# Pieces of 128 columns for GpSimd's two-input operations in an RWKV-7 scan, and a group norm with three DVE operations fewer

## The chip, the cores and the metric

The kernel runs on one core of one Trainium2 chip. The metric is the device time of one execution in microseconds. Its engines are named as in the profile: PE (TensorE matmuls), PEld (TensorE weight loads), DVE (VectorE), ACT (ScalarE), POOL (GpSimd), SP (SyncE, which issues the DMAs).

## The reference

A trunk of two layers on 512 tokens of width 2048, in float32. Layer 0 (stick-breaking attention and a pooling mixer) is not touched. Layer 1 is an RWKV-7 time mixing with 32 heads of 64: projections r, k, v, g, a decay w and a rate a, then a recurrence over the tokens, then a group norm over each head's 64 values, a bonus, a gate and an output projection:

```python
def step(state, inp):
    r_t, w_t, k_t, v_t, kk_t, a_t = inp
    sa = jnp.einsum('bhvk,bhk->bhv', state, -kk_t)
    state = (state * w_t[:, :, None, :] + sa[..., None] * (kk_t * a_t)[:, :, None, :]
             + v_t[..., None] * k_t[:, :, None, :])
    return state, jnp.einsum('bhvk,bhk->bhv', state, r_t)
...
mean = jnp.mean(o, axis=-1, keepdims=True)
var = jnp.mean(jnp.square(o - mean), axis=-1, keepdims=True)
o = ((o - mean) * lax.rsqrt(var + GN_EPS)).reshape(B_, S, D) * gn_w + gn_b
bonus = jnp.sum(r * k * r_k, axis=-1, keepdims=True) * v
o = (o + bonus.reshape(B_, S, D)) * jax.nn.silu(g)
return o.astype(x.dtype) @ w_o
```

## The kernel before

The 32 heads are worked on as 16 pairs p; a pair fills the 128 partitions, two heads of 64. The recurrence is cut into 8 chunks of 64 tokens, so that a chunk becomes a few small matrix products and the state passes from chunk to chunk. All of this is in `scan`, which writes the instructions of several pairs interleaved:

- `vproj(p)` computes v of a pair on PE (vps, lines 142 to 144: 48 matmuls of 128x512 in three passes with split operands). Its weights come in four units of 128x512, loaded by `wunit` one unit ahead of their use. `split` turns each into a high part (whi, an ACT cast, line 137) and a low part (wlo = wraw - whi, line 138). From pair 2 on wlo is made by GpSimd, elsewhere by DVE.
- `gprod(p)` makes products of the loaded factors; DVE masks them into Z (line 885).
- `vprep(p)` multiplies v by the bonus on GpSimd (bv, line 900) and clears RS there (line 903).
- `lanes(p)` and `levels(p)` invert 64x64 triangular matrices. Four GpSimd multiplications gather 16x16 blocks out of Z (nd, line 920); a DVE transpose turns them (lt, line 925); then DVE runs 15 steps of a product pr (line 932, t x t columns in step t) and a reduction uc (line 933).
- `chain(p)` is the recurrence: per chunk PE makes xo, DVE and ACT copy it (xs, lines 1021 and 1022), PE makes sa, DVE copies it (RS, line 1026), PE makes s, and DVE makes the new state M (lines 1041 and 1043). ACT copies the output to O (line 1049).
- `post(p)` is the group norm and the gate of a pair: two reductions (lines 1061 and 1068) and tiny 128x8 operations around them (gs, lines 1062 and 1069; and in `rsqrt_eps`, lines 206 to 214: rssgn, rshgn, rstgn, rsygn), the scaling of O, a transpose on PE, the bonus and the gate (gm, lines 1080 and 1081).

The order is written by hand for PE: `slot` runs 12 steps of two chains (pairs p and p + 1) for each pair, and between the steps it takes from a list of due times (`plan`) the next part of the other generators. DVE, ACT, POOL and SP take their instructions in an order that a scheduler makes from this, with the chains first. Each engine runs its own instructions in order. On POOL the wlo stand in one queue with bv, the clearing of RS and the nd of later pairs.

Of the kernel before, what the change touches and what calls it, by code (L numbers as in the profile page):

```python
# [8 lines left out]
F32 = mybir.dt.float32  # L9
F32R = mybir.dt.float32r  # L10
I32 = mybir.dt.int32
AF = mybir.ActivationFunctionType
ALU = mybir.AluOpType
# [4 lines left out]
P = 128  # L18
# [6 lines left out]
GN_EPS = 64e-5  # L25
# [9 lines left out]
class Kernel:  # L35
# [96 lines left out]
                for n, f, at, r in g:  # L132
                    self.vec[n] = v[:, at:at + r]

    def split(self, hi, lo, src, eng=None):

        self.nc.scalar.copy(hi, src)  # L137
        (eng or self.nc.vector).tensor_sub(lo, src, hi.bitcast(F32))  # L138

    def mm3(self, ps, ah, al, bh, bl, start, stop):  # L140
        mm = self.nc.tensor.matmul
# [4 lines left out]
    def wunit(self, ap, a, b, pool=None, bufs=None, eng=None):  # L146

        pool = pool or self.wp
        ww = self.ww
        raw = self.wp.tile([P, ww], F32, tag="wraw", name="wraw", bufs=3)[:, :a * b].rearrange("p (a b) -> p a b", a=a)  # L150
        self.nc.sync.dma_start(raw, ap)
        kw = {"bufs": bufs} if bufs else {}
        hi = pool.tile([P, ww], F32R, tag="whi", name="whi", **kw)[:, :a * b].rearrange("p (a b) -> p a b", a=a)
        lo = pool.tile([P, ww], F32R, tag="wlo", name="wlo", **kw)[:, :a * b].rearrange("p (a b) -> p a b", a=a)
        self.split(hi, lo, raw, eng)
        return hi, lo

    def gemm_a(self, W, c0, xs, evac, kblocks=NK, feed=None):
# [39 lines left out]
            src = y  # L198
        return y

    def rsqrt_eps(self, pool, v, eps, n, name):

        nc = self.nc
        T = lambda tag: pool.tile([P, n], F32, tag=tag, name=tag + name, bufs=2)
        sd, hx, t, y = T("rss"), T("rsh"), T("rst"), T("rsy")
        nc.scalar.activation(sd, v, AF.Sqrt, bias=self.eps[eps])
        nc.vector.tensor_scalar(hx, v, eps, -0.5, ALU.add, ALU.mult)
        nc.vector.reciprocal(sd, sd)
        if n == 1:
            nc.vector.tensor_scalar(t, sd, sd, hx, ALU.mult, ALU.mult)  # L210
        else:
            nc.vector.tensor_mul(t, sd, sd)
            nc.vector.tensor_mul(t, t, hx)
        nc.vector.scalar_tensor_tensor(y, t, 1.5, sd, ALU.add, ALU.mult)
        return y
# [600 lines left out]
    def scan(self, ctx, xv, first, mp, ld, ar_d, bk_d, bc_d, g_d, m_d):  # L816
        nc, tc, i = self.nc, self.tc, self.i
# [8 lines left out]
        tp = ctx.enter_context(tc.tile_pool(name="stmp", bufs=1))  # L826
        Wv, Wo = i["od_w_v"][0], i["od_w_o"][0]
        lo, hi = slice(0, 64), slice(64, 128)
# [17 lines left out]
        def vproj(p):  # L846

            unit = lambda k0: self.wunit(
                Wv[k0 * P:(k0 + 4) * P, p * P:(p + 1) * P].rearrange("(k p) n -> p k n", p=P), 4, P,
                eng=nc.gpsimd if p > 1 else None)  # L850
            ws = first if p == 0 else [unit(0)]
            ps = pv.tile([P, S], F32, tag="v", name="vps")
            for k in range(NK):
                if k % 4 == 0:
                    wh, wl = ws.pop(0)
                    if k + 4 < NK and not ws:
                        ws.append(unit(k + 4))
                self.mm3(ps, wh[:, k % 4, :], wl[:, k % 4, :], xv[k][:, 0, :], xv[k][:, 1, :], k == 0, k == NK - 1)
                if k % 2 and k < NK - 1:
                    yield  # L860
            vT = sets[p]["vT"] = tp.tile([P, S], F32, tag="vT", name="vT")
            nc.scalar.copy(vT, ps)
            yield

        def gprod(p):

            s = sets[p]
            AR = s["AR"] = ld.tile([P, 8, 2, 64], F32, tag="AR", name="AR", bufs=4)
            nc.sync.dma_start(AR.rearrange("p a b c -> p (a b c)"), ar_d[p])
            BK = ld.tile([P, 8, P], F32, tag="BK", name="BK")  # L870
            nc.sync.dma_start(BK.rearrange("p a b -> p (a b)"), bk_d[p])
            yield

            Z = s["Z"] = [st.tile([P, 8, P], F32, tag=f"Z{h}", name=f"Z{h}", bufs=4) for h in range(2)]
            for b in range(2):
                g = [aux("g").rearrange("p (c n) -> p c n", c=4) for _ in range(2)]
                for c in range(4):
                    for h in range(2):
                        mm(g[h][:, c, :], BK[half[h], 4 * b + c, :],
                           AR[half[h], 4 * b + c].rearrange("p a b -> p (a b)"), start=True, stop=True)  # L880
                    if c == 1:
                        yield
                for h in range(2):
                    mk = self.mk[:, 64 * (p % 2):64 * (p % 2) + P]
                    nc.vector.tensor_mul(Z[h][:, 4 * b:4 * b + 4, :], g[h], mk.unsqueeze(1).to_broadcast([P, 4, P]))  # L885
                yield
            BT = s["BT"] = st.tile([P, 8, P], F32, tag="BT", name="BT")
            for b in range(2):
                g = aux("bt")
                for c in range(4):  # L890
                    nc.tensor.transpose(g[:, c * P:(c + 1) * P], BK[:, 4 * b + c, :], self.ident)
                nc.scalar.copy(BT[:, 4 * b:4 * b + 4, :], g.rearrange("p (c n) -> p c n", c=4))
                yield

        def vprep(p):

            s = sets[p]
            bv = s["bv"] = tp.tile([P, S], F32, tag="bv", name="bv", bufs=3)
            nc.sync.dma_start(bv, bc_d[p])
            nc.gpsimd.tensor_mul(bv, s["vT"], bv)  # L900

            RS = s["RS"] = st.tile([P, 8, 2, 64], F32, tag="RS", name="RS", bufs=3)
            nc.gpsimd.memset(RS[half[p % 2]], 0.0)
            yield
            g = aux("vt")
            for t in range(4):
                nc.tensor.transpose(g[:, t * P:(t + 1) * P], s["vT"][:, t * P:(t + 1) * P], self.ident)
            g5 = g.rearrange("p (t h n) -> p t h n", t=4, h=2)
            for par, rows in ((0, lo), (1, hi)):
                nc.scalar.copy(RS[half[1 - p % 2], par::2], g5[rows])  # L910
            yield
# [141 lines left out]
        def post(p):  # L1053

            s = sets[p]
            gt = tp.tile([P, S], F32, tag="ldg", name="ldg")
            nc.sync.dma_start(gt, g_d[p])
            O = s["O"].rearrange("p t h n -> p (t h) n")
            sm = tp.tile([P, 8], F32, tag="gs", name="gs")
            bc = lambda t: t.unsqueeze(2).to_broadcast([P, 8, 64])  # L1060
            nc.vector.tensor_reduce(sm, O, AX.X, ALU.add)
            nc.vector.tensor_scalar(sm, sm, 1.0 / 64, None, ALU.mult)
            yield
            nc.vector.tensor_sub(O, O, bc(sm))
            sq = tp.tile([P, 8, 64], F32, tag="pt", name="gsq")
            nc.scalar.activation(sq, O, AF.Square)
            yield
            nc.vector.tensor_reduce(sm, sq, AX.X, ALU.add)
            nc.vector.tensor_scalar(sm, sm, 1.0 / 64, None, ALU.mult)
            rs = self.rsqrt_eps(tp, sm, GN_EPS, 8, "gn")  # L1070
            yield
            nc.vector.tensor_mul(O, O, bc(rs))
            yield
            g = aux("ot")
            for t in range(4):
                nc.tensor.transpose(g[:, t * P:(t + 1) * P], s["O"][:, t].rearrange("p h n -> p (h n)"), self.ident)
            m = tp.tile([P, S], F32, tag="pt", name="gm")
            nc.scalar.activation(m, g, AF.Identity, scale=self.vec["gw"][:, p:p + 1], bias=self.vec["gb"][:, p:p + 1])
            yield
            nc.vector.tensor_add(m, m, s["bv"])  # L1080
            nc.vector.scalar_tensor_tensor(m, m, 0.5, gt, ALU.mult, ALU.mult)
            if p < 13:
                nc.sync.dma_start(m_d[p], m)
            else:
                t = mixed[p] = mp.tile([P, 2, S], F32R, tag="mx", name="mixed")
                self.split(t[:, 0, :], t[:, 1, :], m)
            yield
# [67 lines left out]
        def plan_pair(base, q, skip=0):  # L1155

            gp = gprod(q)
            next(gp)
            plan(base, gp, 6, *GP)
            plan(base, hurry(lanes(q)) if q == 15 else lanes(q), 18, *LA)  # L1160
            plan(base, hurry(levels(q)) if q == 15 else levels(q), 5, *LV)
            plan(base, vproj(q), 8, *VJ)
            plan(base, vprep(q), 2, *VP)


        v, gp = vproj(0), gprod(0)
# [9 lines left out]
        g1, v = gprod(1), vproj(1)  # L1176
        next(g1)
        run(la)
        for q in range(6):
            next(g1)  # L1180
            if q % 2:
                next(v)
        run(vprep(0))
        la, l0 = lanes(1), levels(0)
        for q in range(10):
# [122 lines left out]
```

## Time and profile before

| what | value |
|---|---|
| runs shown | 2131.53, 2136.67 and 2141.84 us, median 2136.67 |
| the profiled execution's own time | 2133.83 us |
| its span, first to last instruction | 2132.1 us |
| mean granted TensorE clock | 0.991 of full speed |
| layer 1's scan (first and last vps matmul of v to the last chain step) | about 1420 to 1960 us |

A span is read by stage: the shares of the whole span mix layer 0, the projections and the scan. In rows by line, "x15" is the count, then come the busy time in microseconds and the mean duration of one in nanoseconds, then the idle time of the engine just before these instructions and who ended it. In rows in order of time, a start and a length in microseconds stand first, and the idle time before in square brackets. The chain of waits is followed back from the last instruction, at each step to what released it.

### The profile page before, as it was taken

The numbers are of one execution on the slowest core, as the hardware profiler recorded it, in microseconds if no ns is written. First come the engines' busy times: TensorE is split into PE (matmuls) and PEld (weight loads), VectorE is DVE, ScalarE is ACT, GpSimd is POOL, SyncE is SP. The second block draws the span as 40 slices with busy tenths as digits, with TensorE's granted clock in tenths as the row PEclk, the third lists the DMA queues.
The fourth block names the chain that finished last, engine by engine and source line by source line (L and its number), as shares of the span: only waits on it lengthen the run. The fifth ranks groups of instructions, "written<-read, shape, count | busy, mean of one in ns | idle before, by whom it ended". The sixth has DMA issues, their size and how long they took to land. (4 is left out here: it accounts for less than half of the span.)

```text
span 2132.1 us, 33773 instructions
## 1 busy us (share of the span) xinstructions
PE 2036.6 (96%) x13139; PEld 1645.7 (77%) x13139; DVE 1301.0 (61%) x2557; ACT 954.4 (45%) x1663; POOL 268.9 (13%) x334
## 2 busy tenths in 40 slices
PE   8999999999999998999899989999999999989996
PEld 7888888888888897777688768876667676666786
DVE  5334335445333358666777793368888988987336
ACT  3345345333221138555555672254555555564211
POOL 0000000000000000333000030012333333310003
PEclk9999999999999999999999999999999999999998
DMA  5322222333333343455466665322222332333733
GB/s 190 99 70 79 82 77 65 94 99 99 99 105 113 127 170 123 147 177 157 130 235 215 211 210 189 122 80 63 91 87 89 105 104 68 104 109 100 232 104 114
DMA packets 214031, 262.97 MB, mean 123 GB/s; under 512 B 15768, under 2 KB 161776, under 8 KB 213104
## 3 DMA queue, kind: packets, MB, share of 16 engines
q1 hardware_dynamic: 213872, 260.83, 37.6%
q8 instruction: 103, 1.69, 0.3%
q14 instruction: 56, 0.46, 0.1%
HBM read 214.32 MB, written 46.47 MB: 122 GB/s over the span
## 5 line engine op out<-in xcount | busy, mean ns | idle before, releaser
L138 DVE TENSOR_TENSOR wlo<-wraw,whi 128x1024 fp32r<-128x1024 f32 (+1 forms) x268 | 313.8, 1173 | 487.5 <-ACT whi L137 478.5
L137 ACT CAST whi<-wraw 128x1024 fp32r<-128x1024 f32 (+1 forms) x324 | 303.5, 938 | 563.8 <-PE ga L143 318.7
L143 PE MATMUL ga<-mx,whi 128*128 128x512 f32 x768 | 301.9, 393 | 4.1 <-DVE mx L138 4.1
L142 PE MATMUL ga<-mx,whi 128*128 128x512 f32 x768 | 301.1, 393 | 4.5 <-ACT mx L137 4.5
L142 PE MATMUL ga<-x,whi 128*128 128x512 f32 x768 | 301.0, 392 | 0.0
L144 PE MATMUL ga<-mx,wlo 128*128 128x512 f32 x768 | 301.0, 392 | 0.0
L144 PE MATMUL ga<-x,wlo 128*128 128x512 f32 x768 | 299.5, 390 | 0.4 <-DVE wlo L138 0.4
L143 PE MATMUL ga<-x,whi 128*128 128x512 f32 x768 | 299.1, 390 | 0.0
L490 PE MATMUL gb<-wlo,mixed 128*128 128x512 f32 (+1 forms) x576 | 196.8, 343 | 3.1 <-DVE wlo L138 3.1
L488 PE MATMUL gb<-whi,mixed 128*128 128x512 f32 (+1 forms) x576 | 197.4, 343 | 1.8 <-DVE s L439 1.8
L489 PE MATMUL gb<-whi,mixed 128*128 128x512 f32 (+1 forms) x576 | 196.9, 342 | 0.0
L143 PEld LDWEIGHTS ga<-mx,whi 128*128 128x128 f32 x768 | 145.4, 189 | 38.0 <-DVE mx L138 6.9
L142 PEld LDWEIGHTS ga<-mx,whi 128*128 128x128 f32 x768 | 145.1, 189 | 37.9 <-ACT mx L137 5.9
L144 PEld LDWEIGHTS ga<-mx,wlo 128*128 128x128 f32 x768 | 145.3, 189 | 30.9 <-issue 0.3
L144 PEld LDWEIGHTS ga<-x,wlo 128*128 128x128 f32 x768 | 144.2, 188 | 31.2 <-DVE wlo L138 0.9
L142 PEld LDWEIGHTS ga<-x,whi 128*128 128x128 f32 x768 | 144.3, 188 | 29.4 <-ACT whi L137 0.3
L143 PEld LDWEIGHTS ga<-x,whi 128*128 128x128 f32 x768 | 144.3, 188 | 29.1
L490 PEld LDWEIGHTS gb<-wlo,mixed 128*128 128x128 f32 x576 | 109.1, 190 | 16.8 <-DVE wlo L138 4.4
L488 PEld LDWEIGHTS gb<-whi,mixed 128*128 128x128 f32 x576 | 109.1, 190 | 16.0 <-DVE s L439 3.5
L489 PEld LDWEIGHTS gb<-whi,mixed 128*128 128x128 f32 x576 | 109.2, 190 | 12.4
L142 PE MATMUL vps<-mx,whi 128*128 128x512 f32 x256 | 113.3, 443 | 0.0
L138 POOL TENSOR_TENSOR wlo<-wraw,whi 128x512 fp32r<-128x512 f32 x56 | 74.4, 1328 | 256.6 <-ACT whi L137 234.2
(330 smaller groups left out, 3401.0 us busy)
## 6 DMA issues: line engine op xcount, KB each, us to landing
wraw<-in_ev_w_in SPq DMA_DIRECT2D x96, 512.0 KB, 3.6
wraw<-in_ev_w_out SPq DMA_DIRECT2D x32, 512.0 KB, 3.6
wraw<-in_od_w_k SPq DMA_DIRECT2D x32, 512.0 KB, 4.9
wraw<-in_od_w_r SPq DMA_DIRECT2D x32, 512.0 KB, 4.5
wraw<-in_od_w_g SPq DMA_DIRECT2D x32, 512.0 KB, 3.4
wraw<-in_od_w_v SPq DMA_DIRECT2D x64, 256.0 KB, 2.8
ar_d<-pAR SPq DMA_DIRECT2D x16, 512.0 KB, 2.6
bk_d<-pBK SPq DMA_DIRECT2D x16, 512.0 KB, 3.3
```

What stands on the lines that cost most here:

```text
L137: self.nc.scalar.copy(hi, src)
L138: (eng or self.nc.vector).tensor_sub(lo, src, hi.bitcast(F32))
L142: mm(ps, ah, bh, start=start, stop=False)
L143: mm(ps, ah, bl, start=False, stop=False)
L144: mm(ps, al, bh, start=False, stop=stop)
L488: mm(ps, ah, bh, start=start, stop=False)
L489: mm(ps, al, bh, start=False, stop=False)
L490: mm(ps, ah, bl, start=False, stop=stop)
```

## The change

GpSimd's operations with two inputs in the scan are written as pieces of 128 columns: each wlo of the 56 units as four subtractions, and each bv as four multiplications. In the group norm the two scalings of the sums by 1/64 go: the mean's is folded into the centering, which becomes one scalar_tensor_tensor, and the variance's into the scale of the square root on ACT. The half variance rshgn moves from DVE to ACT. DVE loses three instructions of 128x8 per pair, 48 in all; ACT gains 16; POOL has 288 instructions where it had 72. PE's instructions and their order stay the same.

```diff
-    def split(self, hi, lo, src, eng=None):
+    def split(self, hi, lo, src, eng=None, parts=1):
         self.nc.scalar.copy(hi, src)
-        (eng or self.nc.vector).tensor_sub(lo, src, hi.bitcast(F32))
+        n = src.shape[1] // parts
+        for q in range(parts):
+            sl = slice(q * n, q * n + n)
+            (eng or self.nc.vector).tensor_sub(lo[:, sl], src[:, sl], hi[:, sl].bitcast(F32))
...
-        self.split(hi, lo, raw, eng)
+        self.split(hi, lo, raw, eng, a if eng else 1)
...
-    def rsqrt_eps(self, pool, v, eps, n, name):
+    def rsqrt_eps(self, pool, v, eps, n, name, scale=1.0):
...
-        nc.scalar.activation(sd, v, AF.Sqrt, bias=self.eps[eps])
-        nc.vector.tensor_scalar(hx, v, eps, -0.5, ALU.add, ALU.mult)
+        nc.scalar.activation(sd, v, AF.Sqrt, bias=self.eps[eps], scale=scale)
+        if n == 1:
+            nc.vector.tensor_scalar(hx, v, eps, -0.5, ALU.add, ALU.mult)
+        else:
+            nc.scalar.activation(hx, v, AF.Copy, bias=-0.5 * eps, scale=-0.5 * scale)
...
-            nc.gpsimd.tensor_mul(bv, s["vT"], bv)
+            for q in range(4):
+                nc.gpsimd.tensor_mul(bv[:, q * P:q * P + P], s["vT"][:, q * P:q * P + P], bv[:, q * P:q * P + P])
...
             nc.vector.tensor_reduce(sm, O, AX.X, ALU.add)
-            nc.vector.tensor_scalar(sm, sm, 1.0 / 64, None, ALU.mult)
             yield
-            nc.vector.tensor_sub(O, O, bc(sm))
+            nc.vector.scalar_tensor_tensor(O, bc(sm), -1.0 / 64, O, ALU.mult, ALU.add)
...
             nc.vector.tensor_reduce(sm, sq, AX.X, ALU.add)
-            nc.vector.tensor_scalar(sm, sm, 1.0 / 64, None, ALU.mult)
-            rs = self.rsqrt_eps(tp, sm, GN_EPS, 8, "gn")
+            rs = self.rsqrt_eps(tp, sm, GN_EPS, 8, "gn", 1.0 / 64)
```

The scheduler orders DVE, ACT and SP anew around these edits. Three places show it; line numbers of the changed kernel are up to seven higher.

On DVE, in the group norm of a pair in the middle of the scan (gs are the sums, O the output, pr and uc a later pair's inversion, xs a chain step), before:

```order
L1062 TENSOR_SCALAR gs<-gs 128x8
L933 TENSOR_REDUCE uc<-pr 128x10
L1064 TENSOR_TENSOR O<-O,gs 128x512
L1021 COPY xs_10939<-xo 64x64
L1021 COPY xs_10940<-xo 64x64
L932 TENSOR_TENSOR pr<-uc,la 128x11x11
L933 TENSOR_REDUCE uc<-pr 128x11
L1068 TENSOR_REDUCE gs<-gsq 128x8
L932 TENSOR_TENSOR pr<-uc,la 128x12x12
L1069 TENSOR_SCALAR gs<-gs 128x8
L933 TENSOR_REDUCE uc<-pr 128x12
L207 TENSOR_SCALAR rshgn<-gs 128x8
```

and now:

```order
L1070 SCALAR_TENSOR_TENSOR O<-gs,O 128x512
L1028 COPY xs_10939<-xo 64x64
L1028 COPY xs_10940<-xo 64x64
L940 TENSOR_REDUCE uc<-pr 128x10
L939 TENSOR_TENSOR pr<-uc,la 128x11x11
L1074 TENSOR_REDUCE gs<-gsq 128x8
L940 TENSOR_REDUCE uc<-pr 128x11
L939 TENSOR_TENSOR pr<-uc,la 128x12x12
L214 RECIPROCAL rssgn<-rssgn 128x8
L940 TENSOR_REDUCE uc<-pr 128x12
L218 TENSOR_TENSOR rstgn<-rssgn 128x8
```

The three scalings are gone, the reciprocal stands earlier, and the same pr and uc follow each other with other neighbours.

On POOL, from one pair's wlo to the nd of a later pair (Z are the masked products that nd reads), before:

```order
L138 TENSOR_TENSOR wlo<-wraw,whi 128x512
L900 TENSOR_TENSOR bv<-vT,bv 128x512
L138 TENSOR_TENSOR wlo<-wraw,whi 128x512
L903 MEMSET RS 64x1024
L138 TENSOR_TENSOR wlo<-wraw,whi 128x512 x2
L920 TENSOR_TENSOR nd_10937<-Z_12535,md 32x8x2x16 x2
L920 TENSOR_TENSOR nd_10937<-Z_12536,md 32x8x2x16 x2
```

and now:

```order
L141 TENSOR_TENSOR wlo<-wraw,whi 128x128 x4
L907 TENSOR_TENSOR bv<-vT,bv 128x128 x4
L141 TENSOR_TENSOR wlo<-wraw,whi 128x128 x4
L910 MEMSET RS 64x1024
L141 TENSOR_TENSOR wlo<-wraw,whi 128x128 x8
L927 TENSOR_TENSOR nd_10937<-Z_12581,md 32x8x2x16 x2
L927 TENSOR_TENSOR nd_10937<-Z_12582,md 32x8x2x16 x2
```

The order is the same; each operation is four.

On ACT, in the group norm (gsq are the squares, rssgn the root, whi the cast of the next weights), before:

```order
L1066 ACTIVATE gsq<-O 128x512
L1022 COPY xs_10940<-xo 64x64
L1022 COPY xs_10939<-xo 64x64
L137 CAST whi<-wraw 128x512
L206 ACTIVATE rssgn<-gs,eps_77 128x8
L1049 COPY O<-xo 64x128 x2
```

and now:

```order
L1072 ACTIVATE gsq<-O 128x512
L1029 COPY xs_10940<-xo 64x64
L1029 COPY xs_10939<-xo 64x64
L209 ACTIVATE rssgn<-gs,eps_77 128x8
L213 ACTIVATE rshgn<-gs 128x8
L137 CAST whi<-wraw 128x512
L1056 COPY O<-xo 64x128 x2
```

The cast of the weights has moved behind the root, which waits for DVE's second reduction. On SP one load of w_o near the scan's end stands ahead of two loads of ml where it stood behind them.

## Rows read from the trace of the kernel before

**Rows 1.** the page's head and part 1: busy us (share of the span), instructions.

```profile
span 2132.1 us, 33773 instructions
...
PE 2036.6 (96%) x13139; PEld 1645.7 (77%) x13139; DVE 1301.0 (61%) x2557; ACT 954.4 (45%) x1663; POOL 268.9 (13%) x334
```

**Rows 2.** a stretch: length, busy us of PE, PEld, DVE, ACT, POOL; clock, DMA.

```profile
1460.00:1960.00 500.00, 462.68 (x5565) 339.94 (x5566) 428.77 (x1320) 274.33 (x690) 145.19 (x139) 0.99 0.30 93
```

**Rows 3.** chain of waits, 1460 to 1960 us: shares; then start, length, what.

```profile
by line: DVE pr L932 8.3%; DVE M L1041 7.1%; issue 6.2%; DVE uc L933 5.7%; DVE RS L1026 4.8%; DVE Z L885 4.6%; PE vps L142 4.0%; POOL nd L920 3.5%; DVE xs L1021 3.1%; PE vps L143 3.0%; PE vps L144 2.9%; PE s L1032 2.7%; PE xo L1014 2.6%; PE
1580.08 0.65 DVE rshgn L207
...
1669.08 1.15 DVE gs L1069
...
1856.48 1.15 DVE gs L1069
```

**Rows 4.** DVE groups, 1460 to 1960 us: count, busy us, mean ns, idle.

```profile
L932 DVE TENSOR_TENSOR pr<-uc,la 128x225 f32<-128x225 f32 (+14 forms) x211 | 67.5, 320 | 4.8
```

**Rows 5.** the same view with shapes kept apart.

```profile
L1064 DVE TENSOR_TENSOR O<-O,gs 128x512 f32<-128x512 f32 x15 | 10.3, 684 | 0.1
L1081 DVE SCALAR_TENSOR_TENSOR gm<-gm,ldg 128x512 f32<-128x512 f32 x15 | 10.2, 683 | 0.0
...
L932 DVE TENSOR_TENSOR pr<-uc,la 128x81 f32<-128x81 f32 x14 | 9.9, 710 | 0.5
...
L207 DVE TENSOR_SCALAR rshgn<-gs 128x8 f32<-128x8 f32 x15 | 7.0, 469 | 0.1
...
L1069 DVE TENSOR_SCALAR gs<-gs 128x8 f32<-128x8 f32 x15 | 6.7, 449 | 0.1
...
L932 DVE TENSOR_TENSOR pr<-uc,la 128x1 f32<-128x1 f32 x14 | 6.7, 477 | 0.2
...
L933 DVE TENSOR_REDUCE uc<-pr 128x9 f32<-128x81 f32 x14 | 3.4, 240 | 0.4
...
L1062 DVE TENSOR_SCALAR gs<-gs 128x8 f32<-128x8 f32 x15 | 2.5, 164 | 0.0
...
L933 DVE TENSOR_REDUCE uc<-pr 128x1 f32<-128x1 f32 x14 | 1.8, 129 | 0.2
```

**Rows 6.** order of time at 1638 us, GpSimd (POOL), then DVE: start, length, what.

```profile
1638.19 1.26 POOL L138 TENSOR_TENSOR wlo<-wraw,whi 128x512 fp32r<-128x512 f32 x1 [4.23 <-ACT whi L137]
...
1638.31 1.17 DVE L207 TENSOR_SCALAR rshgn<-gs 128x8 f32<-128x8 f32 x1
```

**Rows 7.** GpSimd's two-input groups: ns min/median/max; the last is a mean.

```profile
L138 POOL TENSOR_TENSOR wlo<-wraw,whi x56: 1262/1276/1642, 1457.5 to 1882.8; 128x512 fp32r<-128x512 f32 x56
...
L920 POOL TENSOR_TENSOR nd<-Z,md x64: 718/729/1085, 1428.7 to 1870.2; 32x256 f32<-32x256 f32 x64
...
L1264 POOL TENSOR_TENSOR s<-s,lng 128x256 f32<-128x256 f32 x1 | 1.2, 1192 | 1.8 <-ACT s L1263 1.8
```

**Rows 8.** order of time at 886 us, GpSimd, then DVE.

```profile
886.80 3.46 POOL L666 TENSOR_TENSOR xr<-xr,lng 128x512 f32<-128x512 f32 x2
890.22 3.45 POOL L667 TENSOR_TENSOR xr<-xr,lnb 128x512 f32<-128x512 f32 x2
...
886.71 4.10 DVE L138 TENSOR_TENSOR ml<-mxf,ml 128x512 fp32r<-128x512 f32 x3
```

**Rows 9.** order of time at 1586 us, GpSimd; [idle before <-releaser].

```profile
1586.78 1.28 POOL L138 TENSOR_TENSOR wlo<-wraw,whi 128x512 fp32r<-128x512 f32 x1 [6.08 <-ACT whi L137]
1588.12 1.54 POOL L920 TENSOR_TENSOR nd<-Z,md 32x256 f32<-32x256 f32 x2
1590.68 1.51 POOL L920 TENSOR_TENSOR nd<-Z,md 32x256 f32<-32x256 f32 x2 [1.02 <-DVE Z L885]
```

**Rows 10.** order of time at 1668 us, ScalarE (ACT).

```profile
1668.22 0.62 ACT L137 CAST whi<-wraw 128x512 fp32r<-128x512 f32 x1
1670.26 0.30 ACT L206 ACTIVATE rssgn<-gs,eps 128x8 f32<-128x8 f32 x1 [1.42 <-DVE gs L1069]
```

## The prediction

> **What bounds the kernel now.** I read the page first. Over the whole span PE is busy for 96% and DVE for 61% [rows 1], but that is an average over stages with different limits. The change touches layer 1's scan alone, so the stage has to be read by itself. Between 1460 and 1960 us, 15 of the 16 group norms and nearly the whole scan, DVE is busy for 428.8 us of 500 (86%), with PE at 462.7, ACT at 274.3 and POOL at 145.2 [rows 2]. A busy PE says less: its matmuls are pipelined and their ends are modelled. So the second view is the chain of waits in that stretch [rows 3]. Its biggest lines are DVE's: pr, M, uc, RS and Z hold 8.3, 7.1, 5.7, 4.8 and 4.6% of the time, together 30.5%, while PE's three vps lines hold 9.9%. DVE bounds the scan, with PE close behind it.
>
> The third reading is why DVE is so busy. A scaling of a 128x8 tile takes 164 ns in one place and means of 469 and 449 ns in two others [rows 5]. In order of time one sees why: a GpSimd subtraction of 128x512 runs from 1638.19 for 1.26 us, and the tiny DVE operation that starts at 1638.31 takes 1.17 us, until the GpSimd operation is over [rows 6]. It is blocked, not slow. The same happens to the products pr: at 128x81 they take 710 ns on average where the reduction that reads the same columns takes 240, and at 128x1 477 against 129 [rows 5].
>
> **The change, part by part.** The sum is made against the profiled execution's 2133.83 us, whose span is 2132.1; that is 2.8 us under the median of the runs shown (2136.67).
>
> *Three tiny DVE operations per group norm go.* In the stretch they take 7.0 + 6.7 + 2.5 = 16.2 us for 45 instructions [rows 5]. The chain names nine blocked ones as pieces of their own: one of 0.65 us, four of 1.08 to 1.10 and four of 1.15, so 9.6 us the first, one of gs and the last are shown [rows 3]. They stand on the chain whole: **-9.6 us**. The other 36 cost 36 x 0.164 = 5.9 us of DVE time. What of DVE's time counts I take from pr, which has 8.3% of 500 us = 41.5 us on the chain of its 67.5 us of busy time, 0.61 [rows 3, 4]: **-3.6 us**. The bounds are nothing and the full 5.9.
>
> *The centering becomes a scalar_tensor_tensor* with the same two inputs. Such an operation takes 683 ns at that shape where the tensor_tensor it replaces takes 684 [rows 5]: nothing.
>
> *ACT makes rshgn instead.* Its neighbour on a 128x8 tile takes 0.30 us [rows 10]: 16 x 0.30 = 4.8 us on an engine that is idle for 226 of 500 us [rows 2]. The order of ACT also changes: a whi cast (0.62 us, [rows 10]) now stands behind rssgn and rshgn, and so behind DVE's second reduction. Before, ACT idled for 1.42 us between the two, so the wait existed, with the cast ahead of it. Queued behind it are the copies of O; the cast, and with it the GpSimd subtraction, comes some 1.2 us later. The weights are asked for one unit ahead, so PE, whose wait for a GpSimd wlo is in none of the chain's leading lines [rows 3], has cover. If that cover were gone, each of the 56 would cost what it is late. I count nothing for it. One load of w_o that moves ahead of two loads of ml on SP's queue also counts nothing: it is at the scan's end and early there.
>
> *GpSimd's 72 operations (56 wlo, 16 bv) become 288 of a quarter the columns.* The trace has no two-input operation of 128x128 on GpSimd. A quarter of 1276 ns, 0.32 us, is the low bound; 0.73 us, what nd takes for 32x256, a high one [rows 7]. The line through nd (256 columns) and wlo (512) has 2.1 ns per column and so gives 0.73 - 128 x 0.0021 = 0.46 us. I take 0.46: a run of four is 1.84 us instead of 1.28.
> A page speaks to this: the Trainium skill, Advanced Engine Details and Errata, The Read-Write Bubble, says that small tiles pay a latency per instruction on ScalarE and VectorE, and not on GpSimd. Taken to mean that pieces of 128 columns lose nothing on GpSimd, a piece would be 0.32 us and the sum below -16.8 instead of -13.8. The line through the two rows, with its fixed part of 0.2 us, does not agree; no row of before settles it.
>
> Does DVE get in between two pieces? At 886.80 four GpSimd operations of 128x512 stand end to end, two of 3.46 us and two of 3.45 in all, so 1.73 us each where one alone takes 1.28; three DVE subtractions beside them take 4.10 us in all [rows 8]. Each side waits for one operation of the other and then goes; DVE does not wait for the whole row. So a blocked DVE operation should wait for the rest of one piece, half of 0.46 on average. For pr the waits now are 14 x (710 - 240) + 14 x (477 - 129) ns = 6.6 + 4.9 = 11.5 us [rows 5]; then 28 x 0.23 = 6.4. Saved 5.1, times 0.61: **-3.1 us**. The later subtraction behind the group norm may now meet a pr where it met the tiny operations; half of 15 times 0.23 us, times 0.61: **+1.1 us**.
>
> *What queues behind the pieces on POOL*: the four nd, for which DVE's transpose lt waits, with all of the pair's pr behind it. At 1586.78 a wlo ends 0.06 us before nd starts; 0.56 us more delay the first two nd, but the third waits 1.02 us for a second Z anyway [rows 9], which absorbs it. Where that slack is smaller something is left: 14 pairs x 0.1 us = **+1.4 us**. The RS memset and bv behind other wlo are early.
>
> Sum: -9.6 - 3.6 - 3.1 + 1.1 + 1.4 = **-13.8 us: 2120**.
>
> **The bounds.** Low: all 5.9 us count and no pr ever waits, so -9.6 - 5.9 - 11.5 = -27: 2107. High: pieces of 0.73 with 0.06 between them (two nd take 1.54 us, [rows 9]), 0.79 each. Written with x for a piece, pr saves (11.5 - 14x) x 0.61, the new meetings cost 7.5 x 0.5x x 0.61, and nd is late by 14 x (4x - 1.28 - 0.06 - 1.02); from x = 0.59 up, where nd is late at all, the sum is -53 + 67x, at 0.79 about -0.4: 2133, or 2136 where the runs lie as far above the profile as now.
>
> **The rivals.**
> 1. *PE takes over.* It is busy for 92.5% of the stretch [rows 2] and already on the chain; the wait that DVE no longer causes is then one for vps or for the latency of a chain step. Against it: the chain's five biggest lines of work are DVE's [rows 3]. If a third of the sum passes: -4.6, **2129**. No change that could be measured.
> 2. *Pieces hold DVE off as one run.* Four pieces without a wait between them could keep DVE out for 1.84 us. A blocked pr then waits 0.56 us longer than now: 28 x 0.56 x 0.61 = +9.6 in place of -3.1, and the new meetings cost 7.5 x 0.92 x 0.61 = +4.2; the sum is +2.0: **2136**. Against it stands the alternation at 886 us [rows 8].
> The Trainium skill's GPSIMD Engine Reference, Instruction dispatch, says that a completed Pool instruction does not hold back the next one, whose cores start as soon as each has finished its share; by that rule pieces could overlap without a gap, and this rival is what follows. For whole operations the trace at 886 us does not bear it out.
> 3. *Slower: GpSimd's pieces are dear and nd comes late.* The dearest small row is 1192 ns for 128x256 [rows 7]. At that price a run of four takes 4.8 us, nd is late by 2.4 us per pair after its slack, and -53 + 67x gives +26: **2160**. It decides at x = 0.80 us, where the sum turns positive. Against it: that row stands beside DVE operations that it may have waited for.
>
> **How the numbers follow.** About 0.5%, 10.7 us, is what a measurement of this kernel tells from no change; under 2126 counts as faster. The forecast case gets 0.64: nine blocked operations that are simply gone are hard to lose. Its own range is 2107 to 2128, of which 0.56 lies under 2126 and 0.08 above. PE taking over gets 0.25, the unbroken run 0.05 (both the same within 0.5%), dear pieces 0.06 (slower). So faster 0.56, same 0.38, slower 0.06. The range from 2107 to 2136 takes in the forecast, the first rival and the high bound; the slow one is left out.
>
> **What would show it.** In the changed profile: between 1460 and 1960 us or the stretch that answers to it, no 128x8 scaling on DVE over 0.2 us; pr at 128x81 under 500 ns; wlo pieces near 0.46 us and in none over 1 us without a DVE operation beside it; DVE's idle time before lt no more than 0.2 us per pair above now; each pair of heads about 0.9 us shorter. The prediction is wrong if DVE's busy time falls by some 20 us and the span does not follow (first rival), if pr at 128x81 still takes 700 ns (second), or if the nd wait grows by over 1 us per pair (third).

## The result, and the profile after

| | before | after |
|---|---|---|
| median of 4 runs (range), us | 2137.39 (2131.53 to 2141.84) | 2115.2 (2114.91 to 2115.52) |
| ratio, 95% interval | | 0.9892 [0.9874, 0.991] |
| the profiled execution, us | 2133.83 | 2115.26 |

The change makes the kernel 1.1% faster: 22 us between the medians, 18.6 between the two profiled executions. The forecast was 13.8 less than the profiled execution of before, 2120. The page's head, which answers to [rows 1]; POOL's whole count goes from 334 to 550, since the 72 and 288 of the change are its wlo and bv alone:

```profile
span 2113.5 us, 33984 instructions
...
PE 2030.0 (96%) x13139; PEld 1644.4 (78%) x13139; DVE 1273.6 (60%) x2509; ACT 954.4 (45%) x1679; POOL 301.1 (14%) x550
```

The time went out of the scan. To compare it between kernels I take it from the first to the last of ACT's 128 copies of O, since these are the same work in each. They start at 1464.5 and 1960.9 us before, and now, in the view of the tile O (count, ns min/median/max, first and last start):

```profile
L1056 ACT COPY O<-xo x128: 243/260/265, 1466.0 to 1940.8; 64x128 f32<-64x128 f32 x128
```

The windows that this gives, of before and then of after (columns as in [rows 2]):

```profile
1464.50:1961.20 496.70, 459.70 (x5536) 337.99 (x5537) 426.10 (x1314) 272.90 (x687) 142.78 (x138) 0.99 0.30 94
```

```profile
1466.00:1941.10 475.10, 452.12 (x5534) 334.82 (x5535) 401.18 (x1269) 272.84 (x702) 174.04 (x344) 0.99 0.32 99
```

The scan is 21.6 us shorter; 1.5 us each come back ahead of it and behind it. DVE's busy time falls by 24.9 us, its idle time rises from 70.6 to 73.9, at one and the same clock of 0.99. DVE's groups, 1460 to 1940 us, against [rows 4], and by shape against [rows 5]:

```profile
L939 DVE TENSOR_TENSOR pr<-uc,la 128x196 f32<-128x196 f32 (+14 forms) x212 | 55.3, 261 | 5.3
```

```profile
L1070 DVE SCALAR_TENSOR_TENSOR O<-gs,O 128x512 f32<-128x512 f32 x15 | 10.3, 684 | 0.0
...
L939 DVE TENSOR_TENSOR pr<-uc,la 128x81 f32<-128x81 f32 x14 | 5.1, 366 | 0.5
...
L219 DVE TENSOR_TENSOR rstgn<-rstgn,rshgn 128x8 f32<-128x8 f32 x15 | 3.4, 230 | 0.3
...
L939 DVE TENSOR_TENSOR pr<-uc,la 128x1 f32<-128x1 f32 x14 | 2.3, 165 | 0.2
```

The group pr lost 12.2 us. The 128x81 product went from 710 to 366 ns, the 128x1 from 477 to 165. The three 128x8 operations of [rows 5] (16.2 us) are gone from DVE; the centering costs the same 684 ns. GpSimd's groups, to be held against [rows 7] (nd has two inputs as well and stays whole):

```profile
L141 POOL TENSOR_TENSOR wlo<-wraw,whi 128x128 fp32r<-128x128 f32 x224 | 100.3, 478 | 219.2 <-ACT whi L137 194.4 <-DVE RS L1033 16.2 <-PE s L1039 4.6
L927 POOL TENSOR_TENSOR nd<-Z,md 32x256 f32<-32x256 f32 x64 | 47.1, 736 | 19.9 <-DVE Z L891 17.1
```

A piece takes 478 ns on average. In order of time, GpSimd and then DVE, at the place where [rows 6] had the blocked operation:

```profile
1628.07 1.70 POOL L141 TENSOR_TENSOR wlo<-wraw,whi 128x128 fp32r<-128x128 f32 x4 [3.58 <-ACT whi L137]
```

```profile
1627.94 0.61 DVE L1033 COPY RS<-sa 64x128 f32<-64x128 f32 x2
1628.58 0.46 DVE L939 TENSOR_TENSOR pr<-uc,la 128x81 f32<-128x81 f32 x1
1629.07 0.41 DVE L1003 TENSOR_TENSOR U<-U,c 32x256 f32<-32x256 f32 x1
```

pr starts 0.51 us into a run of four pieces that goes on to 1629.77. It takes 0.46 us, against 0.24 for the reduction of the same columns, and is done at 1629.04: by these times it waited for the rest of one piece and not of four. The chain of waits, 1460 to 1940 us, has PE's vps ahead of DVE's lines [rows 3]:

```profile
by line: PE vps L145 7.4%; DVE pr L939 5.7%; PE vps L146 5.6%; PE vps L147 5.2%; DVE uc L940 4.5%; issue 4.2%; PE xo L1021 4.2%; PE s L1039 3.5%; DVE M L1048 3.4%; DVE RS L1033 3.4%; PE q L977 3.1%; PE g L885 3.1%; DVE xs L1028 2.4%; PE sa 
```

And DVE's waits in the scan (us in total, times, longest), of before and then of after; RS waited 7.1 us before, tb 1.1:

```profile
DVE lt L925 <- POOL nd L920: 24.2, 14, 2.7
```

```profile
DVE lt L932 <- POOL nd L927: 25.1, 14, 3.6
DVE RS L1033 <- PE sa L1032: 10.5, 14, 2.1
DVE xs L1028 <- PE xo L1024: 5.9, 7, 2.7
DVE tb L948 <- ACT e L946: 2.2, 8, 1.0
```

### The profile page after: what moved, and what is told of

Its sections match the earlier page's. It is cut to its first block, busy times and chain, and to the rows that moved or that the text cites. A ratio compares the mean times of both kernels' runs of the same rounds, so it can differ in the third digit from the quotient of the medians.

```text
span 2113.5 us, 33984 instructions
## 1 busy us (share of the span) xinstructions
PE 2030.0 (96%) x13139; PEld 1644.4 (78%) x13139; DVE 1273.6 (60%) x2509; ACT 954.4 (45%) x1679; POOL 301.1 (14%) x550
## 5 line engine op out<-in xcount | busy, mean ns | idle before, releaser
L141 POOL TENSOR_TENSOR wlo<-wraw,whi 128x128 fp32r<-128x128 f32 x224 | 100.3, 478 | 219.2 <-ACT whi L137 194.4
```

The lines of the kernel that those rows point to most:

```text
L141: (eng or self.nc.vector).tensor_sub(lo[:, sl], src[:, sl], hi[:, sl].bitcast(F32))
```

## The experiments

Theory A: a DVE operation that meets a two-input operation of GpSimd is held until that one operation is over, so the cost goes with the length of a single GpSimd operation, and the pieces bring the gain. Theory B: the gain is that of the instructions that DVE no longer has, and the pieces bring little. All results, in us; the scan and DVE's share of it are read as above (copies of O, windows). The kernel before was timed again beside the experiments, with medians of 2137.03 to 2138.97, and each ratio is to the runs beside it. Two profiled executions of the changed kernel have scans of 475.1 and 476.8, so a difference under 2 us in that column says nothing. The code of the experiments is shown in part, as edits to the changed kernel; "..." marks what is left out.

| kernel | median (range) | ratio [95%] | scan | DVE busy | idle |
|---|---|---|---|---|---|
| before | | | 496.7 | 426.1 | 70.6 |
| the change | 2115.2 (2114.9 to 2115.5) | 0.9892 [0.9874, 0.991] | 475.1 | 401.2 | 73.9 |
| e1 pieces alone | 2114.6 (2110.0 to 2119.7) | 0.9898 [0.9875, 0.9921] | 476.7 | 406.4 | 70.3 |
| e2 norm alone | 2124.6 (2119.3 to 2130.5) | 0.9945 [0.9928, 0.9962] | 486.1 | 413.3 | 72.8 |
| e3 two pieces of 256 | 2120.35 (2118.8 to 2126.1) | 0.9933 [0.9916, 0.995] | 482.0 | 408.6 | 73.4 |
| e4 eight pieces of 64 | 2119.42 (2118.0 to 2125.9) | 0.9926 [0.9908, 0.9943] | 482.4 | 402.5 | 79.9 |
| e5 rshgn on DVE | 2115.74 (2114.0 to 2122.2) | 0.9899 [0.9878, 0.9919] | 476.2 | 401.8 | 74.4 |
| e6 no low part | 2111.55 (2107.9 to 2115.9) | 0.9874 [0.9855, 0.9893] | 473.2 | 397.9 | 75.3 |
| e7 pieces everywhere | 2142.91 (2137.7 to 2147.1) | 1.0023 [1.0011, 1.0035] | 475.4 | 400.6 | 74.8 |
| e8 two nd on DVE | 2115.95 (2114.8 to 2116.4) | 0.9893 [0.9879, 0.9908] | 479.8 | 421.1 | 58.7 |
| e9 pieces, mean fold | 2114.49 (2113.6 to 2118.8) | 0.9891 [0.9875, 0.9908] | 476.9 | 404.3 | 72.6 |
| e10 pieces, variance fold | 2111.78 (2110.3 to 2114.2) | 0.9874 [0.986, 0.9889] | 474.9 | 402.9 | 72.0 |
| e11 the change again | 2113.97 (2112.7 to 2117.8) | 0.9896 [0.9879, 0.9912] | 476.8 | 400.7 | 76.1 |
| e12 as e10, again | 2113.94 (2111.3 to 2119.2) | 0.9893 [0.9874, 0.9911] | 475.9 | 403.5 | 72.4 |

**Which half brings it: e1 and e2.** e1 keeps the pieces and takes the norm back, e2 the reverse:

```diff
...
+            nc.vector.tensor_scalar(sm, sm, 1.0 / 64, None, ALU.mult)
...
-            nc.vector.scalar_tensor_tensor(O, bc(sm), -1.0 / 64, O, ALU.mult, ALU.add)
+            nc.vector.tensor_sub(O, O, bc(sm))
...
```

```diff
-        self.split(hi, lo, raw, eng, a if eng else 1)
+        self.split(hi, lo, raw, eng)
...
```

> The pieces alone, the group norm as before (three tiny operations per pair stay on DVE). Theory A (a DVE operation that reads two SBUF tensors, or scales an SBUF tile, is held until the GpSimd operation it meets is over, so the cost goes with the length of one GpSimd operation): the gs and rshgn that took 1.1 us now take 0.16 to 0.6, pr at 128x81 near 0.35, DVE's busy time in the scan falls by 13 to 17 us and the time to 2119 to 2127. Theory B (what pays is that 48 DVE instructions are gone; the pieces only move the waits): no gain, 2132 to 2138.

> The group norm's edits alone, GpSimd's operations whole. Theory A: the tiny operations' waits go, but the subtraction that held them comes later and holds a pr or a remaining tiny operation instead, for up to 1 us; pr at 128x81 stays near 0.7 us; time 2122 to 2131. Theory B: the whole gain, 2114 to 2118.

The pieces alone give the whole gain, more than either theory expected (2119 to 2127 by A). In e1 PE, DVE, ACT and SP run the same instructions in the same order as before, and only GpSimd's differ. The scan with its busy times, and pr as a whole:

```profile
1461.00:1937.70 476.70, 453.57 (x5536) 335.75 (x5537) 406.36 (x1314) 271.89 (x687) 175.29 (x344) 0.99 0.31 98
```

```profile
L936 DVE TENSOR_TENSOR pr<-uc,la 128x1 f32<-128x1 f32 (+14 forms) x210 | 55.8, 266 | 4.8
```

The tiny operations stand on DVE and cost little (by shape, 1460 to 1940 us); L1073 and rshgn took 449 and 469 ns before, L1066 164:

```profile
L1073 DVE TENSOR_SCALAR gs<-gs 128x8 f32<-128x8 f32 x15 | 2.7, 181 | 0.1
L1066 DVE TENSOR_SCALAR gs<-gs 128x8 f32<-128x8 f32 x16 | 3.0, 189 | 0.0
L210 DVE TENSOR_SCALAR rshgn<-gs 128x8 f32<-128x8 f32 x15 | 2.6, 174 | 0.1
```

e2, inside A's range, has none of the three operations left to hold, and pr is held as before:

```profile
L938 DVE TENSOR_TENSOR pr<-uc,la 128x81 f32<-128x81 f32 x14 | 10.0, 713 | 0.5
...
L938 DVE TENSOR_TENSOR pr<-uc,la 128x1 f32<-128x1 f32 x14 | 5.6, 398 | 0.2
```

The scan falls by 20.0 us with the pieces alone, 10.6 with the norm alone, 21.6 with both: the two halves take away largely the same waits. Theory B falls.

The holding can be seen one operation at a time. Before, GpSimd and then DVE, in order of time:

```profile
1662.69 1.27 POOL L138 TENSOR_TENSOR wlo<-wraw,whi 128x512 fp32r<-128x512 f32 x1 [3.74 <-DVE RS L1026]
```

```profile
1662.80 1.26 DVE L932 TENSOR_TENSOR pr<-uc,la 128x81 f32<-128x81 f32 x1
```

Of the 128x81 pr of before, eight begin inside a wlo, 0.11 to 0.52 us after its start; each ends 98 to 105 ns after that wlo does. In the change eight begin about 0.1 us into a piece, and each ends 99 to 103 ns after that one piece. Those that meet nothing take 246 ns. Not every DVE operation is held: in the change RS takes 289 ns on average whether it begins beside a piece of wlo (67 times) or beside nothing (47), and M 277 and 284. Both read a result of PE from PSUM, while pr has both inputs in SBUF; no run tests whether that is what decides.

**How long may one be: e3 and e4.** Two pieces of 256 columns, and eight of 64, for wlo and bv:

```diff
-        self.split(hi, lo, raw, eng, a if eng else 1)
+        self.split(hi, lo, raw, eng, a // 2 if eng else 1)
...
```

```diff
...
+                for c in (slice(0, 64), slice(64, 128)):
+                    eng.tensor_sub(lo[:, sl, c], src[:, sl, c], hi[:, sl, c].bitcast(F32))
...
```

> The change with two pieces of 256 columns in place of four of 128. Theory A: one piece takes 0.73 us (by the line through 0.46 for 128 and 1.28 for 512 columns), the longest wait is 0.6 us, the sum of DVE's waits lies between that of the change (about 4 us) and that of whole operations (about 21 us), near 9; time 2117 to 2122. Theory B: as the change, 2114 to 2117.

> The change with eight pieces of 64 columns. A piece takes 0.33 us by the same line, a run of eight 2.3 us from start to end where four of 128 take 1.7. Theory A alone: DVE's waits under 3 us, time 2113 to 2116. If the length of the run counts (nd stands behind the last wlo on POOL and DVE's lt waits for nd): the wait for nd grows by up to 0.6 us per pair, 14 pairs, so 2116 to 2124.

e3 lies in A's range, e4 in its second one. The view of the tile wlo, in e3 and then in e4:

```profile
L141 POOL TENSOR_TENSOR wlo<-wraw,whi x112: 718/729/1109, 1455.5 to 1869.0; 128x256 fp32r<-128x256 f32 x112
```

```profile
L145 POOL TENSOR_TENSOR wlo<-wraw,whi x448: 311/319/693, 1458.9 to 1872.3; 128x64 fp32r<-128x64 f32 x150
```

With 64, 128, 256 and 512 columns one takes 319, 458, 729 and 1276 ns: 2.1 ns per column and a fixed 0.19 us. Halves leave 7.4 us more of DVE's busy time than the change. Eighths hold DVE hardly more than quarters (402.5), but their fixed part makes POOL late: DVE's idle time is 6.0 us longer, 3.0 of them in lt's wait for nd, 28.1 us where the change has 25.1:

```profile
DVE lt L936 <- POOL nd L931: 28.1, 14, 4.7
```

The scan is 482 us in both; 128 columns is the best of the sizes tried.

**Where the norm's saving goes: e5, e9 to e12.** Beside the pieces, the norm's edit takes another 5.2 us off DVE's busy time (e1 to the change), and 3.6 come back as idle time. e5 puts rshgn back on DVE in one operation; e9 has the pieces and the mean's fold alone, e10 the pieces and the variance's half:

```diff
-            nc.scalar.activation(hx, v, AF.Copy, bias=-0.5 * eps, scale=-0.5 * scale)
+            nc.vector.tensor_scalar(hx, v, eps / scale, -0.5 * scale, ALU.add, ALU.mult)
```

```diff
...
-            rs = self.rsqrt_eps(tp, sm, GN_EPS, 8, "gn", 1.0 / 64)
+            nc.vector.tensor_scalar(sm, sm, 1.0 / 64, None, ALU.mult)
+            rs = self.rsqrt_eps(tp, sm, GN_EPS, 8, "gn")
```

```diff
+            nc.vector.tensor_scalar(sm, sm, 1.0 / 64, None, ALU.mult)
...
-            nc.vector.scalar_tensor_tensor(O, bc(sm), -1.0 / 64, O, ALU.mult, ALU.add)
+            nc.vector.tensor_sub(O, O, bc(sm))
```

> The change with rshgn back on DVE as one tensor_scalar of 128x8 (the scalings by 1/64 stay folded away). If DVE's busy time is what counts: 16 x 0.17 = 2.7 us more of it, 2116 to 2119. If rshgn on ACT delays the copies and casts behind it (DVE's idle time grew by some 3 us beside the removed instructions): that idle time goes back, 2112 to 2115.

> Pieces of 128 columns and the mean's scaling folded into the centering; the variance's scaling and rshgn on DVE as in the kernel before. One 128x8 operation per pair less than with pieces alone, 15 x 0.164 = 2.5 us of DVE's busy time. If the idle time that grew in the scan under the whole change (RS behind sa, tb behind e, U behind DT) comes from the order on ACT, where rshgn and the later cast stand, DVE's idle time stays near the 70.3 us of pieces alone, and the time is 2111 to 2114 us. If it comes from DVE's shorter queue alone (an engine that is done earlier waits longer for PE), idle rises by about what busy falls, and the time is that of pieces alone, 2113 to 2116.

> Pieces of 128 columns and the variance's half of the norm's edit: the scaling by 1/64 in the square root's scale, rshgn on ACT; centering as before, behind its own scaling. Two 128x8 operations per pair less on DVE than with pieces alone, about 30 x 0.16 = 5 us less any waits that pieces had removed. If ACT's order makes the idle time, DVE's idle time in the scan rises to about 74 us as in the whole change and the time is 2114 to 2117; if DVE's shorter queue makes it, idle rises in proportion to the busy time that goes and the time is 2113 to 2116, no different from the run beside it.

e5 missed: the idle time stays (74.4), so rshgn on ACT is not what makes it. e9 came out as its second case has it, DVE's shorter queue: against e1 busy time falls by 2.1 us and idle time rises by 2.3, at 2114.49. e10 missed: it came out below both of its ranges and lower than any other kernel with the subtraction, which asked for the change beside it on one chip:

> The changed kernel itself, beside the version without the centering fold and the same runs of the kernel before. If the fold of the mean costs (its order moves casts and copies on ACT), this stays at 2114 to 2117 us and above every run of the other; if the two are the same, both lie within 1.5 us of each other.

> Pieces and the variance's half of the norm's edit, centering as before, on the same chip as the changed kernel. If the fold of the mean costs, 2110 to 2114 us and below the run beside it by 2 us or more; if not, the same within 1.5 us, and the difference between the calls so far was that of the chip.

The medians are 2113.97 and 2113.94. With the pieces in place the norm's edit, or any part of it, moves the time by less than can be measured; e10's lead was scatter. In all of them idle time rises as busy time falls, and the scan stays at 474.9 to 476.9 us; which part of the norm makes that is not settled.

**What is left to gain, and where pieces cost: e6, e8, e7.** e6 leaves out the low part of v's weights where GpSimd makes it and clears the tile instead; it bounds what the remaining meetings cost.

```diff
+            if eng:
+                eng.memset(lo[:, sl].bitcast(F32), 0.0)
...
```

> The change with the low part of v's weights left out where GpSimd makes it (cleared by a memset, which reads nothing). It shows what is left of DVE's waits for wlo: those of pr, some 2.7 us, should go if only GpSimd operations that read SBUF hold DVE; nd comes up to 0.4 us earlier per pair. Time 2107 to 2113. If a memset holds DVE too, the waits stay at 1 to 2 us and the time at 2110 to 2115.

```profile
L942 DVE TENSOR_TENSOR pr<-uc,la 128x1 f32<-128x1 f32 (+14 forms) x210 | 52.3, 249 | 5.2
```

```profile
L942 DVE TENSOR_TENSOR pr<-uc,la 128x81 f32<-128x81 f32 x14 | 3.4, 246 | 0.5
```

That is pr, as a group and then at 128x81 by shape, with only bv's pieces left in its way: 249 ns against 261 in the change and 320 before. The median is 2 to 4 us under the change's two, with runs that overlap theirs. e8 goes at the largest wait left, lt for nd, by making two of the four nd on DVE:

```diff
-                nc.gpsimd.tensor_mul(nd2[r, :, :16].rearrange("p t (b c) -> p c b t", b=2),
+                (nc.gpsimd if q < 2 else nc.vector).tensor_mul(nd2[r, :, :16].rearrange("p t (b c) -> p c b t", b=2),
```

> The change with two of the four nd multiplications of each pair (those that read the Z that comes last) on DVE instead of GpSimd. DVE stands idle for 25 us in the scan until GpSimd's nd are done. If DVE's busy plus idle time makes the scan: 28 operations of about 0.42 us more, 12 us, against 20 to 24 us of idle time less; time 2103 to 2110. If the two nd left on GpSimd hold DVE's two (both read two SBUF tensors), most of it is given back: 2111 to 2117.

```profile
L927 DVE TENSOR_TENSOR nd<-Z,md 32x256 f32<-32x256 f32 x28 | 17.7, 634 | 0.7
```

```profile
DVE RS L1033 <- PE sa L1032: 13.7, 25, 2.1
DVE xs L1028 <- PE xo L1024: 10.9, 15, 2.7
```

The wait is gone but for 0.5 us, 17.7 us of work have come, and RS and xs wait 8 us more for PE: no gain. e7 cuts GpSimd's operations elsewhere too, in the stage that makes layer 1's input beside the k projection (xr) and in the last layer norm:

```diff
-                nc.gpsimd.tensor_mul(r, r, ln["g"])
-                nc.gpsimd.tensor_add(r, r, ln["b"])
+                for q in range(0, 512, P):
+                    nc.gpsimd.tensor_mul(r[:, q:q + P], r[:, q:q + P], ln["g"][:, q:q + P])
+                for q in range(0, 512, P):
+                    nc.gpsimd.tensor_add(r[:, q:q + P], r[:, q:q + P], ln["b"][:, q:q + P])
...
```

> The change with pieces of 128 columns also in the two other places where GpSimd has two inputs: the token layout beside k's projection (DVE operations there took up to 1.79 us for 0.69) and the last layer norm. Theory A there: some 25 us less of DVE's waiting, but PE sets the time of that stage, so no gain from it; at the end of the kernel two DVE operations waited 0.8 us each, so 1 to 2 us: 2112 to 2115. If DVE's waits count in k's projection as they do in the scan: 2095 to 2105.

A miss: some 27 us slower than the change, at the same scan. The stretch from 880 to 1060 us, of before and then of e7:

```profile
880.00:1060.00 180.00, 171.33 (x741) 135.81 (x740) 125.41 (x152) 96.90 (x151) 48.27 (x42) 0.98 0.50 154
```

```profile
880.00:1060.00 180.00, 154.81 (x629) 120.36 (x628) 96.65 (x118) 89.43 (x141) 84.76 (x124) 0.91 0.44 139
```

GpSimd's groups (whole execution) and SP's waits (880 to 1060 us) in e7:

```profile
L675 POOL TENSOR_TENSOR xr<-xr,lnb 128x128 f32<-128x128 f32 x64 | 47.7, 774 | 0.0
...
L673 POOL TENSOR_TENSOR xr<-xr,lng 128x128 f32<-128x128 f32 x64 | 44.3, 721 | 25.1 <-DMA xr<-xhat_d 25.1
```

```profile
SPq L676 <- POOL xr L675: 68.9, 13, 8.2
```

The same of before:

```profile
L667 POOL TENSOR_TENSOR xr<-xr,lnb 128x512 f32<-128x512 f32 x16 | 27.1, 1708 | 0.3
L666 POOL TENSOR_TENSOR xr<-xr,lng 128x512 f32<-128x512 f32 x16 | 24.8, 1566 | 25.2 <-DMA xr<-xhat_d 25.2
```

```profile
SPq L668 <- POOL xr L667: 50.4, 14, 7.1
```

Where these pieces run, DVE's operations follow each other without a break (ml, sqr, mxf and wlo, eight operations from 889.59 to 896.91 us beside eight pieces, for one). Of xr's 128 pieces 59 take 447 to 468 ns, as in the scan; the other 69 take 0.68 to 1.48 us, most of them 0.9, and every one of these overlaps a DVE operation. So the means are 721 and 774 ns. xr takes 92 us where it took 52, SP's store behind it waits 18.5 us longer, and the loads queued behind that store come late (in the same 180 us PE waits 23.2 us for the squares ssq, 7.9 before; that the store is the cause is read from these waits and not tested). PE is busy for 154.8 of these 180 us, where before it was busy for 171.3. It stands idle five times for 3.1 to 8.0 us, each time until a ssq, where before it did once, and beside or right after each of these its granted clock falls to the lower of its two levels (1.2 GHz): 0.91 on average over the stretch, 0.98 before. v's first vps starts 26 us later than before. The last layer norm adds some 5 us: from the last copy of O to the end e7 takes 177.2 us, the change 172.4.

## Why the prediction was right, and where it was off

The direction, the stage and the mechanism were right, and 2115.2 lies in the range. The sum was 8 us short on the scan (13.8 against 21.6), and its parts were weighted wrongly. The range is 29 us wide and holds e2's 2124.6 as well, the norm without pieces: that the total lies in it says little for the division of the sum.

- *Three tiny operations go* (-9.6 and -3.6, together -13.2). Alone they give 10.6 us on the scan and 12.4 between medians (e2): right, a little high.
- *pr's shorter waits* (5.1 us, times 0.61, **-3.1**): the term that was mis-sized. Behind the norm's edit the pieces were put at -3.1 + 1.1 + 1.4 = -0.6; measured they are worth 11.0 (e2 to the change). Two steps of it failed. "14 x (710 - 240) + 14 x (477 - 129)" counted two shapes as all that was held and left each still meeting half a piece, 6.4 us in all: 5.1 us saved. The two shapes alone gave back 9.2 us (9.9 to 5.1 and 6.7 to 2.3); what they still wait is 14 x (366 - 246) + 14 x (165 - 151) ns = 1.9 us against e6, not 6.4: at 128x1 pr begins 0.28 to 0.40 us into a piece and waits next to nothing. The other shapes gave 3.0, so the whole group lost 12.2, and e6 shows its floor at 52.3 of the 67.5. And the factor 0.61, pr's share of the chain: of DVE's 24.9 us, 21.6 reached the scan, 0.87. The chain is one path through the old timing; on an engine that is busy for 86% of a stretch and runs its queue in order, an operation off the path still delays those on it. That reason is argued; what is shown is that idle time rose by 3.3 us only. Nor is 0.87 a constant: of the norm's 5.2 us behind the pieces 1.6 reached the scan, less than can be told from nothing.
- *The later meetings* (+1.1): the forecast was a pr that meets the later subtraction. What is met is the tiny operation rstgn behind rshgn, which now takes 230 ns where it took 165, 15 x 65 ns = 1.0 us. Right in size, by luck.
- *nd behind the longer run* (+1.4): lt waits 25.1 us where it waited 24.2, so +0.9.
- *The piece* (0.46): 478 ns on average, a run of four 1.70 us. The reading of the Trainium skill's Advanced Engine Details and Errata, The Read-Write Bubble, by which pieces lose nothing on GpSimd, gave 0.32; the four sizes with their fixed 0.19 us do not bear it out.
- *ACT's order and SP's load* (nothing): e1 has neither and takes the same time.
- *PE takes over* (rival 1): the chain is led by vps now, yet 0.87 passed, not a third. It holds for what comes next: the norm behind the pieces, and e8.
- *Pieces as one run* (rival 2): the pr at 1628.58 goes between two pieces, and pr fell from 320 to 261 ns, where this rival had it rise. The four pieces do stand without a gap (1.70 us for four), yet DVE gets in. The rule of the Trainium skill's GPSIMD Engine Reference, Instruction dispatch, as read there would have kept it out. What fits is the Trainium skill's SBUF — State Buffer, Terms: DVE and GpSimd arbitrate for one shared port pair, which is held for a full instruction while the other engine is blocked. The trace agrees for pr, which ends 0.1 us after the one piece that it met.
- *Dear pieces* (rival 3): not in the scan. In e7 they cost 0.72 to 0.77 us on average, and there the time did get worse.

The marks named ahead were met: pr at 128x81 is under 500 ns, no piece takes over 0.82 us, lt's wait grew by 0.06 us a pair, and each pair is 1.35 us shorter (21.6 / 16) where 0.9 was asked.

## What to carry to other kernels

Where a busy DVE shares a stage with two-input operations on GpSimd, compare a DVE group's mean with that of an equal shape that meets none; in this scan the surplus went with the length of one GpSimd operation, and cutting that operation gave most of it back without touching DVE. Cut only where GpSimd has time to spare: each piece pays a fixed part (0.19 us here), and beside an unbroken DVE often a turn of waiting too (e7), which matters if someone waits for GpSimd's result. Price a saving on the engine that bounds a stretch by its busy time and the idle time that may follow, not by its share of one chain; expect less of the next saving, when another engine leads the chain.

## What was not expected of the hardware

- A memset on GpSimd (202 ns on average for 128x128) did not hold DVE's pr: in e6 the nine of 128x64 that begin beside one take 225 ns on average, the four that meet nothing 226.
- The waiting goes both ways: a two-input piece of 128x128 on GpSimd has a median of 458 ns in the scan and means of 721 and 774 beside the k projection.
- The change's first four runs lay within 0.6 us; the same kernel later spread over 5 us (2112.68 to 2117.76), as the other kernels do. That was chance and no property of the change.
